# One 512-wide value product per key block, compressed logits joined to the window's last matmul, and gates kept as their inverses

## Chip, cores and metric

The kernel runs on one core of one Trainium2 chip. The metric is the time on the device in microseconds (us) of one execution; the times below are those of the kernel before, and the profile is of one further execution. TensorE is called PE, VectorE DVE, ScalarE ACT, GpSimd POOL, SyncE SP.

## What is computed

A transformer block over 1,024 tokens of width 1,024, in fp32: RMS norm, one projection (`w_in`), an mLSTM mixer and a sparse-attention mixer side by side, two gated branch products, an output product, and a gated feed-forward part. The change lies in the attention mixer, whose core is, for each block of queries:

```python
lc  = einsum(qb, kc_) + bias           # 63 compressed keys
p_c = masked_softmax(lc, ...);   o_c = einsum(p_c, vc_)
ls  = einsum(qb, k_g) + bias_s         # selected blocks: all keys up to the query
p_s = masked_softmax(ls, ...);   o_s = einsum(p_s, v_g)
lw  = einsum(qb, k_wb) + bias          # window of 512 keys
p_w = masked_softmax(lw, ...);   o_w = einsum(p_w, v_wb)
out = gb[0] * o_c + gb[1] * o_s + gb[2] * o_w     # gb = sigmoid(gate_in)
```

With 1,024 tokens and 16 blocks to select out of 16, "selected" means every key up to the query. There are 8 heads of width 64 in two groups of four; a group shares its keys and values.

## The kernel before

**Split numbers.** PE multiplies in a short format (fp32r), so fp32 operands are cut into a high part (a copy rounded to fp32r) and a low part (the rest). Projections take three matmuls per 128 rows of the contraction (`mm3`: high*high, high*low, low*high), each 512 columns wide. In the attention the two parts of the queries stand above one another in one tile (`QA`, 64 rows each), as do copies of the keys (`KH`, `KL`), so logits take two matmuls: `QA` with `KH`, then with `KL`. The values carry both parts side by side (`VHL`, and `VHC` for the compressed ones), so that rows 0 to 63 of the output are the product with the high part and rows 64 to 127 with the low part.

**Stages around the change.** B2 (about 313 to 383 us of the span) makes the queries: four tiles `nq`, each two halves of 24 matmuls, evicted by ACT (`snq`), cut by DVE (`hnq`, `lnq`) and stored through SP (`d_qh`, `d_ql`). Beside it `compress` makes the compressed keys `KHC`, `KLC` and values `VHC`. After the first tile, `load_pair(0)` loads what the attention of the first two heads needs: the queries `QA` and the keys `KH`, `KL` through POOL's DMA queue, the bias rows `FB`, `FW` through SP's. SP also loads the raw weights of the tiles to come (`raw`), and the compression's second weights (`w`).

C (383 to 708 us) is the attention. A unit is one pair of heads `p` and one block of 128 queries `i`; 32 units run, `i` in the order 0, 7, 1, 6, 2, 5, 3, 4 for each `p`. Per unit:

- `s_job`: logits of the window (`w`, up to 5 blocks of 128 keys), of the compressed keys (`c`, both heads in one job), of the selected keys (`s`, i+1 blocks). Each job takes one of two PSUM tiles `S` of two banks; DVE adds the bias and takes the row's extreme (`low`), ACT takes exp and the row sum (`exp`).
- `scale`: DVE makes gate / sum (`rs`: maximum, reciprocal, product with the gate `GT`), then DVE or ACT multiplies the rows with it.
- `t_job`: PE transposes two blocks of both heads into PSUM (`T`), ACT copies the high part out (`TH`), DVE subtracts for the low part (`TL`), and `pv` multiplies: per block one matmul with `TH`, one with `TL`, 256 columns each, summed in one half of the bank `obank`; units alternate between the halves.
- `out_copy`: ACT copies the 128 x 256 sums out (`os`), SP stores them to `d_yn`.

The order of all this is written by a planner in the kernel's own code (`Op`, `queues`, `ready`), which simulates PE, ACT and DVE with assumed durations; where PE would stand still for more than 120 ns it inserts a step of three matmuls (`d`) of the merge tiles, projections that need nothing of the attention. Nine of the sixteen merge tiles lie in C. `load_pair` for the next pair is called when the last logits of a pair are done; K tiles change only between pairs 1 and 2.

D (from 708 us) first makes the seven merge tiles left, 10.9 us each. Within them `load_y` is stepped, four steps to a tile: it loads `d_ym` and `d_yn` through SP, DVE adds the two `d_yn` sources (high and low values), ACT and DVE cut the sum into `YH` and `YL`, the operands of the branch products that begin at 785 us. In each tile ACT also evicts two halves and, in the fourth step, copies the next tile's weights (`whi`); POOL subtracts (`wlo`). Every engine's queue is in order.

Of the kernel before, what the change touches and what calls it, by code (L numbers as in the profile page):

```python
# [14 lines left out]
P = 128  # L15
T = 1024
# [15 lines left out]
FX = 1152  # L32
NEG = -1.0e30
# [124 lines left out]
def body(ctx, tc, a, out, stop=None, dbg=None):  # L158
# [45 lines left out]
    d_yn = [[tc.dram_tile([P, T], F32, name=f"d_yn{z}{j}") for j in range(4)] for z in range(2)]  # L204
# [137 lines left out]
    with ExitStack() as sa:  # L342
# [222 lines left out]
        def gates():  # L565
# [69 lines left out]
            nc.scalar.activation(GT[:, :, 0:24], GT[:, :, 0:24], AF.Sigmoid)  # L635
            nc.scalar.preload_act_table_set(EXPLN)
# [167 lines left out]

    def load_pair(p):
# [27 lines left out]
    with ExitStack() as sb:  # L833
# [73 lines left out]
        driver(b2_dense(), compress())  # L907
        if "VHC" in dbg:
# [9 lines left out]
    def merge_tile(j, sp, psp, bufs, tag="mg", tbufs=2):  # L918
# [8 lines left out]
    with ExitStack() as sc:  # L927
# [14 lines left out]
        def s_job(u, kind, r):  # L942
# [10 lines left out]
            if kind == "c":  # L953
                n8, nn = 8 * i + 8, ncmp(i)
                e = cp.tile([P, 2, P], F32, name=f"E{u}c", tag="Ec", bufs=3)
                nc.gpsimd.memset(e[:, :, nn:P], 0.0)
                EX[u, "c"] = e
                for q in range(2):
                    o = s[:, 64 * q:64 * q + n8]
                    nc.tensor.matmul(o, QA[2 * p + q][:, cs], KHC[:, g, 0:n8], start=True, stop=False)  # L960
                    nc.tensor.matmul(o, QA[2 * p + q][:, cs], KLC[:, g, 0:n8], start=False, stop=True)
                y0 = 31 + 16 * (56 - 8 * i)
                rows_ = [(e[:, q, 0:nn], s[:, 64 * q:64 * q + nn], FB[2 * p + q][:, y0:y0 + 16 * (nn - 1) + 1:16], q, 0)
                         for q in range(2)]
                cost = 4 * 107.0
            else:
                b = 1 if kind == "s" else 2
                n, k0 = (P * (i + 1), 0) if b == 1 else (P * nwin(i), P * max(0, i - 4))
                kh, kl = KS[g, b - 1]
                q_ = QA[2 * p + r]  # L970
                cost = 0.0
                for c0 in range(0, n, 512):
                    m = min(512, n - c0)
                    nc.tensor.matmul(s[:, c0:c0 + m], q_[:, cs], kh[:, k0 + c0:k0 + c0 + m], start=True, stop=False)
                    nc.tensor.matmul(s[:, c0:c0 + m], q_[:, cs], kl[:, k0 + c0:k0 + c0 + m], start=False, stop=True)
                    cost += 2 * max(107.0, m / 2.4)
                e = cp.tile([P, T if b == 1 else 640], F32, name=f"E{u}{kind}{r}", tag="E" + kind, bufs=4)
                EX[u, kind, r] = e
                if b == 1 or i < 4:
                    bias = FB[2 * p + r][:, 896 - P * i:896 - P * i + n]  # L980
                else:
# [938 lines left out]
```

## Time and profile before

| | |
|---|---|
| three runs | 1622.4 us median (1619.43 to 1623.4) |
| profiled execution, its time | 1624.57 us |
| its span, first to last instruction | 1622.8 us |
| PE, DVE, ACT busy in the span | 97%, 66%, 46% |
| PE, DVE, ACT busy in C | 98%, 83%, 79% |
| mean granted PE clock | 0.991 |

Busy shares of PE count matmuls that overlap, so the distance from one matmul's start to the next is the better measure of its cost. The feed-forward part after D is not touched.

### The profile page before, as it was taken

The numbers are of one execution on the slowest core, as the hardware profiler recorded it, in microseconds if no ns is written. First come the engines' busy times: TensorE is split into PE (matmuls) and PEld (weight loads), VectorE is DVE, ScalarE is ACT, GpSimd is POOL, SyncE is SP. The second block draws the span as 40 slices with busy tenths as digits, with TensorE's granted clock in tenths as the row PEclk, the third lists the DMA queues.
The fourth block names the chain that finished last, engine by engine and source line by source line (L and its number), as shares of the span: only waits on it lengthen the run. The fifth ranks groups of instructions, "written<-read, shape, count | busy, mean of one in ns | idle before, by whom it ended". The sixth has DMA issues, their size and how long they took to land.

```text
span 1622.8 us, 22113 instructions
## 1 busy us (share of the span) xinstructions
PE 1572.2 (97%) x7938; PEld 1327.5 (82%) x7938; DVE 1066.4 (66%) x2276; ACT 746.6 (46%) x1561; POOL 204.5 (13%) x225
## 2 busy tenths in 40 slices
PE   6999999989999999999999998999999999999997
PEld 6876888878989888988887887888888888888876
DVE  6456553245888687952355378666676666978996
ACT  5225455325878687853334344333333333454443
POOL 4002333310102110012000014000000000000130
PEclk9999999999999999999999999999999999999999
DMA  8003532782233422154447222222332223741202
GB/s 251 7 22 97 150 116 96 240 242 70 67 101 82 125 66 82 40 173 148 143 139 255 74 85 85 78 87 89 118 103 78 79 78 104 285 166 42 98 7 104
DMA packets 143773, 181.43 MB, mean 112 GB/s; under 512 B 10414, under 2 KB 100944, under 8 KB 143664
## 3 DMA queue, kind: packets, MB, share of 16 engines
q1 hardware_dynamic: 137440, 157.31, 31.5%
q0 software_dynamic: 5888, 22.06, 4.8%
q8 instruction: 62, 1.02, 0.3%
q10 hardware_dynamic: 336, 0.66, 0.1%
q14 instruction: 47, 0.39, 0.1%
HBM read 137.95 MB, written 49.90 MB: 116 GB/s over the span
## 4 chain that ended last, share of the span: by engine, by line
PE 82%; DVE 4%; DMA 3%; ACT 1%; issue 1%; SPq 0%; POOL 0%; DVEq 0%; ACTq 0%
PE PS L271 14%; PE PS L272 14%; PE PS L270 14%; PE d L270 6%; PE d L272 6%; PE d L271 6%; PE T L1043 4%; PE obank L1063 2%; PE obank L1065 2%; PE br L270 1%; PE br L271 1%; PE br L272 1%; DMA raw<-in_w_in 1%; PE pn L696 1%; DMA q<-d_yn 0%
## 5 line engine op out<-in xcount | busy, mean ns | idle before, releaser
L270 PE MATMUL d<-UTH,whi 128*128 128x512 f32 x576 | 235.1, 408 | 3.4 <-ACT snq L846 2.4
L272 PE MATMUL d<-UTH,wlo 128*128 128x512 f32 x576 | 227.1, 394 | 1.1 <-POOL wlo L249 1.1
L271 PE MATMUL d<-UTL,whi 128*128 128x512 f32 x576 | 226.1, 393 | 0.0
L1421 DVE TENSOR_TENSOR sl<-PS,sl 128x512 f32<-128x512 f32 x182 | 124.0, 688 | 100.2 <-PE PS L272 98.4
L272 PEld LDWEIGHTS d<-UTH,wlo 128*128 128x128 f32 x576 | 108.9, 189 | 26.1 <-POOL wlo L249 1.9
L270 PEld LDWEIGHTS d<-UTH,whi 128*128 128x128 f32 x576 | 109.2, 190 | 21.9 <-ACT snq L846 3.0
L249 POOL TENSOR_TENSOR wlo<-raw,whi 128x1024 fp32r<-128x1024 f32 x31 | 76.2, 2458 | 402.5 <-ACT whi L247 308.2
L271 PEld LDWEIGHTS d<-UTL,whi 128*128 128x128 f32 x576 | 109.6, 190 | 17.6
L1052 DVE TENSOR_TENSOR TL<-T,TH 128x512 fp32r<-128x512 f32 (+1 forms) x184 | 103.7, 583 | 20.9 <-ACT TH L1048 19.5
L1048 ACT ACTIVATE TH<-T 128x512 fp32r<-128x512 f32 (+1 forms) x184 | 90.8, 511 | 34.4 <-PE T L1043 31.6
L1421 DVE TENSOR_TENSOR sl<-sl,sl 128x512 f32<-128x512 f32 (+1 forms) x113 | 77.3, 691 | 18.3 <-ACT sl L1424 12.9
L1424 ACT ACTIVATE sl<-sl 128x512 f32<-128x512 f32 (+1 forms) x85 | 53.5, 631 | 69.8 <-PE PS L271 47.6
L1063 PE MATMUL obank<-TH,VHL 128*128 128x256 f32 x264 | 76.4, 312 | 0.0
L1424 ACT ACTIVATE wh<-sl 128x512 fp32r<-128x512 f32 x61 | 38.5, 631 | 81.9 <-PE PS L271 71.6
L1421 POOL TENSOR_TENSOR acc<-acc 128x512 f32<-128x512 f32 x6 | 9.2, 1548 | 503.5 <-DVE acc L1421 503.4
L1065 PE MATMUL obank<-TL,VHL 128*128 128x256 f32 x264 | 68.5, 282 | 0.0
L270 PE MATMUL PS<-q 128*128 128x512 f32 x172 | 66.9, 389 | 0.0
L271 PE MATMUL PS<-q 128*128 128x512 f32 x172 | 66.9, 389 | 0.0
L272 PE MATMUL PS<-q 128*128 128x512 f32 x172 | 66.9, 389 | 0.0
L1383 DVE TENSOR_TENSOR q<-br,q 128x512 f32<-128x512 f32 x32 | 21.9, 688 | 67.3 <-ACT q L1376 47.0
L1424 ACT ACTIVATE q<-sl 128x512 fp32r<-128x512 f32 x74 | 43.4, 624 | 46.5 <-PE PS L271 29.1
L1421 DVE TENSOR_TENSOR q<-sl,q 128x512 fp32r<-128x512 f32 x72 | 50.3, 736 | 2.9 <-ACT q L1424 2.9
(1418 smaller groups left out, 4302.0 us busy)
## 6 DMA issues: line engine op xcount, KB each, us to landing
raw<-in_w_in SPq DMA_DIRECT2D x40, 512.0 KB, 4.7
ra<-in_w_gate SPq DMA_DIRECT2D x22, 512.0 KB, 5.3
d_gu<-sl SPq DMA_DIRECT2D x44, 256.0 KB, 2.1
q<-d_mg SPq DMA_DIRECT2D x32, 256.0 KB, 3.2
d_rep<-d_row POOLq DMA_DIRECT2D x8, 960.0 KB, 10.0
sl<-d_gu SPq DMA_DIRECT2D x15, 512.0 KB, 5.3
sl<-in_w_down SPq DMA_DIRECT2D x15, 512.0 KB, 5.2
ra<-in_w_up SPq DMA_DIRECT2D x11, 512.0 KB, 3.8
```

The costliest lines, as they stand in the source:

```text
L249: eng.tensor_tensor(lo, v, cast32(hi), ALU.subtract)
L270: nc.tensor.matmul(ps, ah, bh, start=first, stop=False)
L271: nc.tensor.matmul(ps, ah, bl, start=False, stop=False)
L272: nc.tensor.matmul(ps, al, bh, start=False, stop=last)
L1043: nc.tensor.transpose(pt[:, z, P * r:P * r + P], e, ident)
L1048: nc.scalar.activation(hl[0][:, 0:m], pt[:, 0:m], AF.Copy)
L1052: nc.vector.tensor_tensor(hl[1][:, 0:m], pt[:, 0:m], cast32(hl[0])[:, 0:m], ALU.subtract)
L1063: nc.tensor.matmul(po, vv, th[:, z, :], start=(st[1] == 0), stop=False)
L1065: nc.tensor.matmul(po, vv, tl[:, z, :], start=False, stop=(st[1] == st[2]))
L1383: nc.vector.tensor_tensor(sg[b], ps, sg[b], ALU.mult)
L1421: return pl.step(alts, lambda e: ENG[e].tensor_tensor(out_(), x(), y(), alu), reads, writes, **kw)
L1424: return pl.step((("ACT", cost),), lambda e: nc.scalar.activation(out_(), x(), fn), reads, writes, **kw)
```

## The change

- **Value product.** High and low parts stand side by side in one tile `TT` [block, high or low, 256]. `pv` does one matmul of 512 columns per block. The output is now 128 x 512 and fills the bank, so all units take turns with it: the first `pv` of a unit depends on the `out_copy` of the unit before (was: two before). `os` is 512 wide in one buffer (was three of 256), `d_yn` doubles to 8 MB, and `load_y` sums four sources instead of two, in 16 half tiles of 512 columns instead of 8 tiles of 1,024 (10 steps become 18).
- **Compressed logits.** The K tiles of the window (`KH1`, `KL1`) are laid out in blocks of 192: 128 keys, then the 64 compressed keys of the group, repeated behind each block by POOL (`behind`). The last matmul pair of a window job is 192 wide, and its tail is the compressed logits. The `c` job is gone. K loads for these two tiles write pieces of 128 elements instead of whole rows of 1,024.
- **Gates.** `GT` is inverted once; `rs` is one maximum-and-product and one reciprocal, two DVE operations instead of three.
- **Room.** `sl` and `st` in B2 and `mg` in C go from two buffers to one.
- The planner's assumed durations follow.

```diff
+KB = 192
-    d_yn = [[tc.dram_tile([P, T], F32, name=f"d_yn{z}{j}") for j in range(4)] for z in range(2)]
+    d_yn = [[tc.dram_tile([2 * P, T], F32, name=f"d_yn{z}{j}") for j in range(4)] for z in range(2)]
...
+            nc.vector.reciprocal(GT[:, :, 0:24], GT[:, :, 0:24])
...
+    def behind(g):
+
+        for t_, c_ in zip(KS[g, 1], (KHC, KLC)):
+            nc.gpsimd.tensor_copy(t_[:, :, P:KB], c_[:, g, None, :].to_broadcast([P, NT, KB - P]))
...
-                kh = kq.tile([P, T], F32R, name=f"KH{g}{j}", tag=f"KH{j}", bufs=1)
+                m = KB if j == 1 else P
+                kh = kq.tile([P, NT, m], F32R, name=f"KH{g}{j}", tag=f"KH{j}", bufs=1)
...
-                nc.gpsimd.dma_start(kh[0:64, :], d_kh[j][gs, :])
...
+                for t_, d_ in ((kh, d_kh), (kl, d_kl)):
+                    for z in range(2):
+                        nc.gpsimd.dma_start(t_[64 * z:64 * z + 64, :, 0:P], d_[j][gs, :].rearrange("p (b c) -> p b c", c=P))
...
+            if g > 0:
+                behind(g)
...
-                    lo = bp.tile([P, 512], F32R, name=f"l{nm}{j}{half}", tag="sl", bufs=2)
-                    st = bp.tile([P, 512], F32, name=f"s{nm}{j}{half}", tag="st", bufs=2)
+                    lo = bp.tile([P, 512], F32R, name=f"l{nm}{j}{half}", tag="sl", bufs=1)
+                    st = bp.tile([P, 512], F32, name=f"s{nm}{j}{half}", tag="st", bufs=1)
...
+                nw = nwin(i)
+                n, o0 = P * nw, P if nw == 4 else 0
+                if nw > 1:
+                    logits(s[:, o0:o0 + n - P], lambda k: k[:, i + 1 - nw:i, 0:P], False)
+                logits(s[:, o0 + n - P:o0 + n - P + KB], lambda k: k[:, i, :], True)
...
-                nc.vector.tensor_scalar(rs, sm, 1.0e-30, None, ALU.max)
+                nc.vector.scalar_tensor_tensor(rs, sm, 1.0e-30, gt, ALU.max, ALU.mult)
                 nc.vector.reciprocal(rs, rs)
-                nc.vector.tensor_tensor(rs, rs, gt, ALU.mult)
...
-                    nc.tensor.matmul(po, vv, th[:, z, :], start=(st[1] == 0), stop=False)
                     st[1] += 1
-                    nc.tensor.matmul(po, vv, tl[:, z, :], start=False, stop=(st[1] == st[2]))
+                    nc.tensor.matmul(obank, vv, hl[0][:, z].rearrange("p x c -> p (x c)"), start=(st[1] == 1), stop=(st[1] == st[2]))
...
-                if first and u >= 2:
-                    dp.append(("OC", u - 2))
+                if first and u >= 1:
+                    dp.append(("OC", u - 1))
...
-            for k in range(10):
+            for k in range(18):
...
+                for src in ([d_ym[j]] if j < 4 else [d_yn[z][j - 4][P * x:P * x + P, :] for x in range(2) for z in range(2)]) if j < 8 else []:
```

How the order of instructions moves, at three places. The first is PE at the start of C: `S0w`, `S0c`, `S0s` are the logits of unit 0, `d` is a merge tile. Before:

```order
L974 MATMUL S0w_3228<-KH_2880,QA_2874 128x128
L975 MATMUL S0w_3228<-KL_2881,QA_2874 128x128
L974 MATMUL S0w_3232<-KH_2880,QA_2877 128x128
L975 MATMUL S0w_3232<-KL_2881,QA_2877 128x128
L270 MATMUL d_0_3210<-UTH,whi_3128 128x512
L271 MATMUL d_0_3210<-UTL,whi_3128 128x512
L272 MATMUL d_0_3210<-UTH,wlo_3129 128x512
L960 MATMUL S0c_3245<-KHC,QA_2874 128x8
L961 MATMUL S0c_3245<-KLC,QA_2874 128x8
L960 MATMUL S0c_3245<-KHC,QA_2877 128x8
L961 MATMUL S0c_3245<-KLC,QA_2877 128x8
L974 MATMUL S0s_3253<-KH_2886,QA_2874 128x128
```

The same place on PE now:

```order
L971 MATMUL S0w_3231<-KH_2881,QA_2875 128x192
L972 MATMUL S0w_3231<-KL_2882,QA_2875 128x192
L971 MATMUL S0w_3237<-KH_2881,QA_2878 128x192
L972 MATMUL S0w_3237<-KL_2882,QA_2878 128x192
L271 MATMUL d_0_3213<-UTH,whi_3129 128x512
L272 MATMUL d_0_3213<-UTL,whi_3129 128x512
L273 MATMUL d_0_3213<-UTH,wlo_3130 128x512
L971 MATMUL S0s_3253<-KH_2887,QA_2875 128x128
L972 MATMUL S0s_3253<-KL_2888,QA_2875 128x128
```

The four `c` matmuls are gone, and the window's last pair grows from 128 to 192 columns.

The second place is PE between the last two units: the transposes (`T`) of unit 31 and its first value product (`obank`). Before, the products of unit 31 go into the other half of the bank:

```order
L1043 MATMUL T_1_7696<-cst,E31w_7522 128x128
L1043 MATMUL T_1_7696<-cst,E31w_7565 128x128
L1043 MATMUL T_1_7696<-cst,E31w_7522 128x128
L1043 MATMUL T_1_7696<-cst,E31w_7565 128x128
L270 MATMUL d_1_7434<-UTH,whi_6711 128x512
L271 MATMUL d_1_7434<-UTL,whi_6711 128x512
L272 MATMUL d_1_7434<-UTH,wlo_6712 128x512
L1043 MATMUL T_2_7715<-cst,E31w_7522 128x128
L1043 MATMUL T_2_7715<-cst,E31w_7565 128x128
L1063 MATMUL obank<-TH_0_7701,VHL 128x256
L1065 MATMUL obank<-TL_0_7711,VHL 128x256
```

Now, where the first row is unit 30's last product and the last row unit 31's first, which waits for the copy of the bank:

```order
L1071 MATMUL obank<-TT_4_7051,VHL 128x512 x2
L1053 MATMUL T_1_7074<-cst,E31w_6896 128x128
L1053 MATMUL T_1_7074<-cst,E31w_6908 128x128
L1053 MATMUL T_1_7074<-cst,E31w_6896 128x128
L1053 MATMUL T_1_7074<-cst,E31w_6908 128x128
L271 MATMUL d_1_7083<-UTH,whi_6488 128x512
L272 MATMUL d_1_7083<-UTL,whi_6488 128x512
L273 MATMUL d_1_7083<-UTH,wlo_6489 128x512
L1053 MATMUL T_2_7089<-cst,E31w_6896 128x128
L1053 MATMUL T_2_7089<-cst,E31w_6908 128x128
L1071 MATMUL obank<-TT_0_7072,VHL 128x512 x2
```

Six transposes and one step of `d` stand between the two. After unit 31's last product 12 matmuls of `d` are left now; before, none was.

The third place is ACT in D: the merge tiles' evictions (`q` from `d`), the copies `YH`, and the next tile's weights (`whi`). Before, all of `load_y` ends within the third of the seven tiles:

```order
L266 ACTIVATE YH<-q_0_2_7808 128x512 x2
L247 ACTIVATE whi_7897<-raw_7802 128x1024
L266 ACTIVATE YH<-q_0_2_7808 128x512 x2
L922 ACTIVATE q_5_0_7789<-d_0_7873,COLS 128x512
L266 ACTIVATE YH<-q_1_3_7809 128x512 x2
L266 ACTIVATE YH<-q_4_1_7807 128x512 x2
L922 ACTIVATE q_5_0_7789<-d_1_7918,COLS 128x512
L266 ACTIVATE YH<-q_0_2_7808 128x512 x2
L247 ACTIVATE whi_7982<-raw_7877 128x1024
L266 ACTIVATE YH<-q_1_3_7809 128x512 x2
```

Now it ends in the fifth; these are the rows of the fourth and the fifth:

```order
L267 ACTIVATE YH<-q_0_2_7189 128x512
L248 ACTIVATE whi_7439<-raw_7326 128x1024
L267 ACTIVATE YH<-q_1_3_7190 128x512
L932 ACTIVATE q_5_0_7170<-d_0_7412,COLS 128x512
L267 ACTIVATE YH<-q_4_1_7188 128x512
L267 ACTIVATE YH<-q_0_2_7189 128x512
L932 ACTIVATE q_5_0_7170<-d_1_7463,COLS 128x512
L267 ACTIVATE YH<-q_1_3_7190 128x512
L248 ACTIVATE whi_7531<-raw_7416 128x1024
L267 ACTIVATE YH<-q_4_1_7188 128x512
```

Two `whi` now stand behind copies of sums of four (the third and the seventh of the eight such half tiles); before, one stood behind the third of the four sums of two.

## Rows read from the trace of the kernel before

**Rows 1.** Windows: stretch, busy us of each engine (instructions), PE clock, DMA share, GB/s.

```profile
358.00:369.00 11.00, 7.25 (x23) 5.59 (x23) 6.97 (x21) 1.06 (x1) 0.00 (x0) 0.53 0.84 241
383.00:708.00 325.00, 317.98 (x2121) 285.26 (x2120) 270.36 (x904) 257.11 (x675) 37.29 (x61) 1.00 0.30 75
708.00:785.00 77.00, 76.33 (x337) 62.87 (x336) 18.14 (x20) 23.69 (x37) 17.51 (x7) 1.00 0.55 176
```

**Rows 2.** Timeline of PE in C: start us, us, engine, line, tile, shape.

```profile
521.42 0.28 PE L1065 MATMUL obank<-TL,VHL 128*128 128x256 f32 x1
...
522.13 0.28 PE L1065 MATMUL obank<-TL,VHL 128*128 128x256 f32 x1
...
522.61 0.27 PE L960 MATMUL S15c<-KHC,QA 128*128 128x40 f32 x1
...
523.06 0.37 PE L1063 MATMUL obank<-TH,VHL 128*128 128x256 f32 x1
...
524.51 0.22 PE L974 MATMUL S15s<-KH,QA 128*128 128x128 f32 x1
...
524.68 0.45 PE L974 MATMUL S15s<-KH,QA 128*128 128x512 f32 x1
...
526.09 0.39 PE L270 MATMUL d<-UTH,whi 128*128 128x512 f32 x1
...
526.55 0.40 PE L272 MATMUL d<-UTH,wlo 128*128 128x512 f32 x1
```

**Rows 3.** The bank's instructions: count, ns min/median/max, first and last start.

```profile
L1063 PE MATMUL obank<-TH,VHL x264: 277/283/368, 389.7 to 706.2; 128*128 128x256 f32 x132
```

**Rows 4.** Groups by line in C: busy us, mean ns, idle before.

```profile
L1005 DVE TENSOR_TENSOR rs<-rs,GT 128x4 f32<-128x4 f32 x64 | 12.8, 199 | 2.2
```

**Rows 5.** Timelines of PE and ACT at C's end; idle before and releaser in brackets.

```profile
702.20 0.41 PE L1043 MATMUL T<-cst,E31c 128*128 128x128 f32 x2 [0.72 <-DVE TL L1052]
...
706.30 0.38 PE L1065 MATMUL obank<-TL,VHL 128*128 128x256 f32 x1
...
706.72 0.38 ACT L1071 ACTIVATE os<-obank 128x256 f32<-128x256 f32 x1 [0.93 <-PE obank L1065]
...
707.16 0.50 PE L270 MATMUL d<-UTH,whi 128*128 128x512 f32 x1 [0.47 <-ACT os L1071]
```

**Rows 6.** B2: two pieces of the ending chain, then timelines of ACT and PE.

```profile
334.25 21.21 DMA raw<-in_w_in
...
359.46 4.61 DMA w<-in_w_cmp
...
355.48 1.06 ACT L247 ACTIVATE whi<-raw 128x1024 fp32r<-128x1024 f32 x1 [8.90 <-DMA raw<-in_w_in]
...
357.34 0.50 PE L270 MATMUL d<-UTH,whi 128*128 128x512 f32 x1 [1.94 <-ACT snq L846]
...
364.20 1.19 PE L887 MATMUL ph<-fl,w 128*128 128x126 f32 x4 [3.75 <-DMA w<-in_w_cmp]
```

**Rows 7.** DMA queues from 338 to 348 us: packets, MB, share of 16 engines.

```profile
q0 software_dynamic: 625, 2.06, 84.2%
q1 hardware_dynamic: 822, 0.56, 42.4%
```

**Rows 8.** The store of `d_ql` issued at 338.0 us: us from issue to landing.

```profile
DMA to landing us min/median/max: 18.7/18.7/18.7
```

**Rows 9.** D: timelines of DVE, POOL and PE, and a DMA issue (KB, us to landing).

```profile
728.32 1.22 DVE L1354 TENSOR_TENSOR q<-q 128x1024 f32<-128x1024 f32 x1 [3.56 <-DMA q<-d_yn]
...
731.46 1.22 DVE L1354 TENSOR_TENSOR q<-q 128x1024 f32<-128x1024 f32 x1
...
738.02 3.16 POOL L249 TENSOR_TENSOR wlo<-raw,whi 128x1024 fp32r<-128x1024 f32 x1 [14.41 <-ACT whi L247]
...
741.23 0.50 PE L272 MATMUL d<-UTH,wlo 128*128 128x512 f32 x1 [0.67 <-POOL wlo L249]
...
q<-d_yn SPq DMA_DIRECT2D x8, 512.0 KB, 7.2
```

More of the change, by code (lines that the diff above doesn't have):

```diff
@@ L907, in body @@
         driver(b2_dense(), compress())
+        behind(0)
         if "VHC" in dbg:
@@ L952, in s_job @@
             s = psC.tile([P, T], F32, name=f"S{u}{kind}{r}", tag="S", bufs=2)
[L953 to L961, printed above, removed]
-                y0 = 31 + 16 * (56 - 8 * i)
[L963 to L981, printed above, removed]
-                    bias = FW[2 * p + r]
-                rows_ = [(e[:, 0:n], s[:, 0:n], bias, r, b)]
@@ new lines, in s_job, with logits @@
+            b = 1 if kind == "s" else 2
+            kh, kl = KS[g, b - 1]
+            q_ = QA[2 * p + r]
+            e = cp.tile([P, T if b == 1 else 640], F32, name=f"E{u}{kind}{r}", tag="E" + kind, bufs=4)
+            EX[u, kind, r] = e
+            f = FB[2 * p + r]
+            def logits(o, k_, last):
+                nc.tensor.matmul(o, q_[:, cs], k_(kh), start=True, stop=False)
+                nc.tensor.matmul(o, q_[:, cs], k_(kl), start=False, stop=True)
+            if b == 1:
+                n, o0 = P * (i + 1), 0
+                for c0 in range(0, i + 1, 4):
+                    m = min(4, i + 1 - c0)
+                    logits(s[:, P * c0:P * (c0 + m)], lambda k: k[:, c0:c0 + m, :], False)
+                rows_ = []
+            else:
+                nw = nwin(i)
[3 more added lines that the diff above has]
+                logits(s[:, o0 + n - P:o0 + n - P + KB], lambda k: k[:, i, :], True)
+                if r == 0:
+                    EX[u, "c"] = cp.tile([P, 2, P], F32, name=f"E{u}c", tag="Ec", bufs=3)
+                ec, nn = EX[u, "c"], ncmp(i)
+                nc.gpsimd.memset(ec[:, r, nn:P], 0.0)
+                y0 = 31 + 16 * (56 - 8 * i)
+                rows_ = [(ec[:, r, 0:nn], s[:, o0 + n:o0 + n + nn], f[:, y0:y0 + 16 * (nn - 1) + 1:16], r, 0)]
@@ L991, in exp @@
                     nc.scalar.activation(e_, e_, AF.Exp, bias=nx[:, q, b:b + 1], scale=-1.0, accum_out=sm[:, q, b:b + 1])
-            return cost, low, exp
+            return low, exp
         def scale(u, part):
@@ L1108, in build_s @@
             ops = {}
-            for k, r in (("w", 0), ("w", 1), ("c", 0), ("s", 0), ("s", 1)):
-                b = {"w": 2, "c": 0, "s": 1}[k]
+            for k, r in (("w", 0), ("w", 1), ("s", 0), ("s", 1)):
+                b = {"w": 2, "s": 1}[k]
                 box = {}
                 def emit(u=u, k=k, r=r, box=box):
-                    _, box["low"], box["exp"] = s_job(u, k, r)
-                n = 126 if k == "c" else (P * (i + 1) if b == 1 else P * nwin(i))
-                cost = 428.0 if k == "c" else 2 * sum(max(107.0, min(512, n - c) / 2.4) for c in range(0, n, 512))
+                    box["low"], box["exp"] = s_job(u, k, r)
+                if b == 1:
+                    n, parts = P * (i + 1), [min(512, P * (i + 1) - c) for c in range(0, P * (i + 1), 512)]
+                else:
+                    n, parts = P * nwin(i), [P * (nwin(i) - 1)] * (nwin(i) > 1) + [KB]
+                cost = 2 * sum(max(109.0, m / 2.4 + 13.0) for m in parts)
                 deps = []
@@ L1242, in place_dense @@
             dstate["gate"] = gate
-        todo_pair = {p: sum(1 for u in range(NU) if units[u][0] == p) * 5 for p in range(4)}
+        todo_pair = {p: sum(1 for u in range(NU) if units[u][0] == p) * 4 for p in range(4)}
         pair_at[0] = 2500.0
@@ L1354, in load_y @@
                         nc.vector.tensor_tensor(y, y, y2, ALU.add)
-                    for half in range(2):
-                        hs = slice(512 * half, 512 * half + 512)
-                        split_evict(YH[:, k - 2, hs], YL[:, k - 2, hs], y[:, hs])
+                    j, hs = (k - 2) // 2, slice(512 * (k % 2), 512 * (k % 2) + 512)
+                    split_evict(YH[:, j, hs], YL[:, j, hs], y)
                 yield
```

54 lines of the change are left out of this document (25 added, 29 removed).

## The prediction, made before the changed kernel ran

> **What bounds the kernel now.** I read the windows by stage first. In C PE is busy 318 of 325 us, DVE 270, ACT 257 [rows 1]. A busy PE counts matmuls that overlap, so I read next, in the timeline, how far apart matmuls start. In a run of value products seven starts lie 0.71 us apart from first to last, 0.118 us for one of 256 columns; 512-wide ones stand 0.23 us apart; the four `c` matmuls of a unit take 0.45 us up to the next product, though only 40 columns wide; a pair of 128-wide logits takes 0.17 us [rows 2]. These starts follow each other almost without gaps, so PE's own work sets C's length, and what is taken from it shortens C, as long as DVE (83%) and ACT (79%) keep up. The waits that remain are few; two sit at C's end, 0.72 and 0.47 us, where the merge steps have run out [rows 5].
>
> Then I followed the ending chain before C. In B2 a raw weight load issued at 334.25 us takes 21.2 us; ACT waits 8.9 us for it, PE 1.94 us for ACT's late eviction, and the second compression weights (`w`) are issued only at 359.46, since SP's queue is in order behind a store of the same late half; PE waits 3.75 us for them [rows 6]. In the 11 us around these waits PE's granted clock is 0.53, that is mostly the lower of its two levels, 1.2 instead of 2.4 GHz, while it stood idle and after [rows 1]. In D the only wait of PE is 0.67 us for `wlo` behind `load_y` [rows 9].
>
> **The change, part by part.**
>
> *Compressed logits.* Gone are 32 jobs of 0.45 us: 14.4 us of PE [rows 2]. Added: no row has a 192-wide pair; it lies between the 128-wide pair, 0.17, and two 256-wide matmuls, 0.24 us; I take 0.20. A 384-wide pair, likewise, lies between 0.24 and 0.46; I take 0.35. Of the 64 window jobs, 32 have five blocks and only swap a 128 for a 192 pair: +0.03 each, 1.0 us. For one to four blocks the job is cut in two where one pair did (0.17, 0.24, 0.35, 0.46 us become 0.20, 0.37, 0.44, 0.55): +0.34 us over the four, eight jobs of each: 2.7 us. Net -10.7 us (-12.5 to -8.2 with the pair at either end).
>
> *Value product.* 264 blocks [rows 3] and one compressed block per unit, 296 in all: 2 x 0.118 becomes 0.23, -2.0 us. One weight load goes, but not the columns, and columns are what is paid here. The Trainium skill ("TensorE: Matmul & The Clock Gate", Back-to-back issue gap) gives about 131 ns for a sustained 512-wide matmul and 81 ns for a 128-wide one. By that the 296 products would cost some 39 us and the gain would be thirty, not two. The dense runs here disagree: 0.23 us between starts [rows 2].
>
> *Turn-taking.* A unit's first product now waits for the copy of the whole bank. Seen at C's end: the last product starts at 706.30, ACT copies from 706.72 for 0.38 us, PE goes on at 707.16, 0.86 us later [rows 5]. With 512 columns the product is 0.11 longer and the copy about 0.6 (256 columns took 0.38, the 1,024-wide `whi` 1.06 [rows 6]), so 1.2 us, of which 0.23 is the product: 0.97 us of other work must stand between. In the new order I counted it at all 31 hand-overs, with the distances above and 0.11 for a transpose: the least is 1.0 us (unit 11), seven have under 1.5, most two to five. That is barely enough at seven places where ACT has something else queued; I take +1 us (0 to +4). Without the cover each would cost some 0.8.
>
> *End of C.* 12 matmuls of merge steps are left over now, so the two waits are filled: -1.2 us.
>
> *Gates, DVE and ACT.* 64 DVE operations of 0.2 us go, 12.8 us [rows 4]. The planner moves 14 row scalings from ACT to DVE (48 on ACT become 34), which ACT needs for copies that are 0.22 longer, 7 us. DVE and ACT both end a few us lower, as PE does: no gain by itself, cover for the rest. The inversion of `GT` is a single small operation in a stage where PE runs projections: nothing. The memsets double on POOL, which is busy 37 of 325 us [rows 1]: nothing.
>
> *K loads and single buffers in B2.* From 338 to 348 us two DMA queues compete: POOL's moved 625 packets of 3.3 KB on average, SP's 822 of 0.7 KB [rows 7]. They alternate nearly packet by packet, so the raw load, in small packets, gets a quarter of the bytes. Now half the K loads come in pieces of 512 bytes (128 elements), eight times as many. Alternating with those, the raw load should move as fast as they: the queries' 1 MB stands ahead of the keys in POOL's queue and is gone after 5 us at 2.06 MB in 10 us, near 343; at 82 packets per us (822 in 10 us) some 600 of the raw load's 1,024 pieces are then left. A small packet held an engine for about 0.08 us (42.4% of 16 engines for 10 us, over 822), so 600 alternating pairs take 4 to 6 us: it would land at 347 to 349 instead of 355.5. ACT's 8.9 us wait and PE's 1.94 us then go. Against it: the single `sl` buffer makes `lnq` wait for the store of the half before, which took 18.7 us [rows 8]; it is queued behind the same raw load and lands as much earlier, near 350, which `lnq` then waits for. The next `lnq` waits for the next store; so `w` is issued about 355 to 357 instead of 359.5, and PE, which would now arrive at 357.3, still waits some 2 to 3 us. Taken together 1.94 plus about 1.3 plus a part of the time lost at the lower clock: I take -4 us. Bounds: -8 if both waits and the low clock go; +3 if the raw load gets no faster and the single buffers delay `w` by another store (3 us).
>
> *K loads between pairs 1 and 2.* The new order has 18 us of PE work between the last logits that read the old keys and the first that read the new, more than the loads and two POOL copies need: nothing.
>
> *load_y.* A whole tile took 3.14 us of DVE and ACT in turn, 1.22 for its one add [rows 9]. A half tile now takes three adds of 0.61, the copy 0.62 and the subtraction 0.65: 3.2 us with hops, eight of them 25.6 us instead of 12.6. A merge tile (10.9 us) holds four, 12.8 us: the chain falls behind PE. The sources are issued after the second tile's last store, near 729.5, and land 7.2 us later [rows 9], at 737. The third copy ends at 745.9; `whi` 1.06, `wlo` 3.16 and hops follow: 750.5, needed at 751.3 (707.16 [rows 5] plus four tiles, plus two matmuls, since `wlo` is used by the third). The seventh ends at 758.7, its `wlo` at 763.3, needed at 762.2: 1.1 us of waiting in place of 0.67. The loads are 2 MB per half merge tile (5.45 us), 390 GB/s where D now moves 176 [rows 1], so they may lag a little. I take +1 us (-0.7 to +6).
>
> Sum: -10.7 - 2.0 + 1 - 1.2 - 4 + 1 = -15.9 us on the profiled execution's 1624.6, or 1608.7. That execution is 2.2 above the median, so on the median 1606.5.
>
> **Rivals.**
> - *B2 gives nothing.* The K loads' small pieces are no help, or the single buffers eat it: 1609 to 1614, 1611 likely. For it: no row shows pieces of 512 bytes in POOL's queue.
> - *DVE or ACT paces C.* PE's starts were dense only because merge steps filled every gap. DVE falls by 12.8 less about 6 for the scalings, so C shortens by some 6 us instead of 13: 1614. Against it: the waits on DVE and ACT in C are short.
> - *`load_y` becomes a wait.* If 8 MB come not in the 21 us that 390 GB/s need but at the 300 or so that the two queues of B2 moved together (2.62 MB in 10 us is 262), the chain ends 5 us later: 1612.
> - *The one bank stalls the units* (the slower side). If ACT reaches the copy late at most hand-overs, each costs up to 0.8 us plus what ACT is behind. Gains and losses balance when the mean uncovered wait over 31 hand-overs reaches about 0.55 us; at 0.8 it gives 1622.4 - 17 + 25 = 1630. Against it: the counted cover.
> - *Wide products overlap.* If a 512-wide product cost no more than a 256-wide one (0.118), 33 us more would go: 1573. That is the direction of the skill's page named above; the dense 512-wide rows speak against it.
>
> **Numbers.** The forecast as summed 0.52, its own range 1601 to 1611; B2 nothing 0.24; DVE or ACT 0.1; `load_y` 0.07; the one bank 0.05; overlap 0.01; no effect 0.01. The range that leaves out two in ten: 1599 to 1616. About 0.3%, 5 us, is what a measurement of this kernel tells from no change. Faster by more than that takes all cases but the bank, no effect and the upper tail of the others: 0.91; same 0.04; slower 0.05.
>
> **What would show it.** C (first `S0w` to the last `os`) 11 to 15 us shorter; products 0.23 apart; no `c` group; the first product of a unit with waits on `os` below 2 us in total; the raw load in B2 landing in 13 us rather than 21, and PE's wait for `w` below 3 us; one wait of PE on `wlo` of 1 us or so in D's sixth tile. The prediction is wrong if PE waits on `os` at most hand-overs, if the raw load still takes 20 us, if the 192-wide pairs cost more than 0.24, or if PE stands for many us at the entry to the branch products.

## The result and the profile after

| | before | after |
|---|---|---|
| median of six runs | 1622.46 us (1619.43 to 1623.4) | 1612.63 us (1610.84 to 1617.35) |
| profiled execution, its span | 1624.57, 1622.8 us | 1610.84, 1609.1 us |
| ratio after/before, 95% interval | | 0.9946, 0.993 to 0.9962 |

The change makes the kernel 9.8 us faster by the medians, 13.7 by the two profiled executions; the forecast was 15.9, that is 1606.5 us with a range of 1599 to 1616. Of the 3.9 us between the two measures, 2.1 are that before's profiled execution lies above its median, and 1.8 that the changed kernel's lies below its own.

By stages of the two traces (first `snq` of B2, first `S0w`, last `os`, first branch product): B2 is 1.8 us shorter (58.6 to 56.8), C 15.4 (323.8 to 308.4), D 4.6 longer (77.7 to 82.4). 12 of the merge matmuls, 2.7 us at 0.227, moved from C to D, so C gained 12.7 net and D lost 1.9. The stages ahead of B2 are 1.1 us shorter, those behind D differ by 0.1; the change doesn't touch them, but for the inversion of `GT` at 127 us, 1.4 us of DVE. "Net of the 12 merge matmuls" below means that these 2.7 us are counted with C.

Windows of the changed kernel: the stretch around the waits of B2, then C, then D (answers to [rows 1]).

```profile
356.00:367.00 11.00, 5.33 (x23) 4.39 (x22) 6.62 (x20) 1.69 (x2) 0.55 (x2) 0.69 0.83 240
380.00:688.00 308.00, 302.85 (x1729) 253.25 (x1728) 264.17 (x854) 249.20 (x658) 40.68 (x93) 1.00 0.39 91
688.00:771.00 83.00, 79.91 (x352) 65.52 (x351) 34.56 (x40) 25.92 (x39) 17.01 (x7) 1.00 0.67 219
```

In C, PE is still busy 98% of the time, and DVE and ACT, with shares of 86% and 81%, are nearer to it than before (83% and 79%). PE's timeline in C (answers to [rows 2]):

```profile
471.81 0.25 PE L971 MATMUL S11w<-KH,QA 128*128 128x192 f32 x1
...
472.01 1.04 PE L1053 MATMUL T<-cst,E9s 128*128 128x128 f32 x8
...
477.83 0.34 PE L971 MATMUL S11s<-KH,QA 128*128 128x384 f32 x1
...
478.18 1.08 PE L1071 MATMUL obank<-TT,VHL 128*128 128x512 f32 x4
479.11 0.60 PE L1053 MATMUL T<-cst,E10w 128*128 128x128 f32 x4
```

The 192-wide pair takes 0.20 us (471.81 to 472.01), the 384-wide pair 0.35, and four products of 512 columns 0.93, 0.23 each: the three prices of the forecast. The bank's instructions, and all waits of PE in C with total, number and longest (answers to [rows 3] and [rows 5]):

```profile
L1071 PE MATMUL obank<-TT,VHL x264: 388/398/506, 386.7 to 688.0; 128*128 128x512 f32 x132
L1078 ACT ACTIVATE os<-obank x32: 578/597/600, 390.2 to 688.4; 128x512 f32<-128x512 f32 x32
```

```profile
PE obank L1071 <- DVE TT L1061: 1.9, 2, 1.3
PE T L1053 <- DVE TT L1061: 1.7, 2, 1.5
PE d L271 <- ACT mg L932: 1.1, 2, 0.8
PE S26w L971 <- DVE nx L998: 0.2, 1, 0.2
```

PE never waits for `os`: the two waits of a product are for DVE's `TT`. (`mg` is ACT's eviction of a merge tile, `nx` DVE's work on the tile of logits before.) A copy of the bank takes 0.60 us, as estimated. Of the three operations of `rs` two are left (answer to [rows 4]):

```profile
L1014 DVE SCALAR_TENSOR_TENSOR rs<-sm,GT 128x4 f32<-128x4 f32 x64 | 12.0, 187 | 3.2 <-ACT E18c L1002 0.7 <-ACT E14c L1002 0.7 <-ACT E23c L1002 0.7
L1015 DVE RECIPROCAL rs<-rs 128x4 f32<-128x4 f32 x64 | 11.2, 174 | 2.2
```

B2, in the ending chain: start, length, what (answers to [rows 6] and [rows 8]); then ACT's split of the raw weights that SP issued at 333.02.

```profile
337.01 11.68 DMA d_ql<-lnq
348.78 0.78 DVE lnq L857
349.58 6.72 DMA d_ql<-lnq
356.40 0.69 DVE lnq L857
357.09 0.25 DVE fl L892
357.49 4.47 DMA w<-in_w_cmp
```

```profile
347.12 1.06 ACT L248 ACTIVATE whi<-raw 128x1024 fp32r<-128x1024 f32 x1 [1.55 <-DMA raw<-in_w_in]
```

The raw load is ready after 14.1 us, not 21.2, and PE's wait of 1.94 us behind ACT is gone. But the chain now runs over two stores: each `lnq` waits until the store of the half before has read the single `lo` buffer. `w` is issued at 357.49, and PE, which comes earlier now, waits 5.7 us for it, not 3.75. The queues from 338 to 348 us (answers to [rows 7]):

```profile
q0 software_dynamic: 1987, 1.75, 104.7%
q1 hardware_dynamic: 1037, 0.91, 47.6%
```

SP's queue moves 0.91 MB where it moved 0.56: 1.9 packets of POOL to one of SP now, where it was 0.8, but smaller ones.

D: PE's two waits, then DVE's chain of adds and POOL's subtraction, at an earlier tile (answers to [rows 9]).

```profile
746.71 0.50 PE L271 MATMUL d<-UTH,whi 128*128 128x512 f32 x1 [1.24 <-ACT whi L248]
...
749.30 0.50 PE L273 MATMUL d<-UTH,wlo 128*128 128x512 f32 x1 [1.85 <-POOL wlo L250]
```

```profile
727.04 2.14 DVE L1366 TENSOR_TENSOR q<-q 128x512 f32<-128x512 f32 x3
729.88 0.69 DVE L268 TENSOR_TENSOR YL<-q,YH 128x512 fp32r<-128x512 f32 x1 [0.70 <-ACT YH L267]
730.49 4.22 DVE L1366 TENSOR_TENSOR q<-q 128x512 f32<-128x512 f32 x3
```

```profile
730.87 2.55 POOL L250 TENSOR_TENSOR wlo<-raw,whi 128x1024 fp32r<-128x1024 f32 x1 [13.38 <-ACT whi L248]
```

Three adds take 2.14 us, but 4.22 when POOL's `wlo` starts among them: the one that starts at 731.21 takes 2.77 us, not 0.69, and ends at 733.98, 0.55 us after POOL. A half tile takes 3.45 us, since DVE also stands 0.70 us for ACT's copy in each. For the loads of `d_yn` DVE waits once in all of D, 2.1 us ahead of the first add.

### The profile page after: what moved, and what is told of

Same layout as the page of the kernel before. It is cut to its first block, busy times and chain, and to the rows that moved or that the text cites. A ratio compares the mean times of both kernels' runs of the same rounds, so it can differ in the third digit from the quotient of the medians.

```text
span 1609.1 us, 21387 instructions
## 1 busy us (share of the span) xinstructions
PE 1557.4 (97%) x7562; PEld 1296.3 (81%) x7562; DVE 1074.7 (67%) x2247; ACT 741.4 (46%) x1547; POOL 209.6 (13%) x261
## 4 chain that ended last, share of the span: by engine, by line
PE 81%; DVE 5%; DMA 3%; ACT 2%; issue 1%; SPq 0%; POOL 0%; DVEq 0%; ACTq 0%
PE PS L271 15%; PE PS L272 15%; PE PS L273 15%; PE d L271 6%; PE d L273 6%; PE d L272 6%; PE obank L1071 4%; PE T L1053 4%; PE br L273 1%; PE br L271 1%; PE br L272 1%; DMA d_ql<-lnq 1%; DVE q L1366 1%; DMA q<-d_yn 1%; PE pn L698 1%
## 5 line engine op out<-in xcount | busy, mean ns | idle before, releaser
L1061 DVE TENSOR_TENSOR TT<-T,TT 128x512 fp32r<-128x512 f32 (+1 forms) x184 | 104.0, 581 | 22.8 <-ACT TT L1058 21.5
L1058 ACT ACTIVATE TT<-T 128x512 fp32r<-128x512 f32 (+1 forms) x184 | 91.2, 510 | 28.9 <-PE T L1053 24.3
L1071 PE MATMUL obank<-TT,VHL 128*128 128x512 f32 x264 | 89.7, 424 | 1.9 <-DVE TT L1061 1.9
L1432 DVE TENSOR_TENSOR wh<-sl,wh 128x512 fp32r<-128x512 f32 x59 | 41.4, 702 | 13.9 <-ACT wh L1435 13.9
```

Of the source, the lines that this page charges most:

```text
L1058: nc.scalar.activation(hl[0][:, 0:m, 0], pt[:, 0:m], AF.Copy)
L1061: nc.vector.tensor_tensor(hl[0][:, 0:m, 1], pt[:, 0:m], cast32(hl[0])[:, 0:m, 0], ALU.subtract)
L1071: nc.tensor.matmul(obank, vv, hl[0][:, z].rearrange("p x c -> p (x c)"), start=(st[1] == 1), stop=(st[1] == st[2]))
L1432: return pl.step(alts, lambda e: ENG[e].tensor_tensor(out_(), x(), y(), alu), reads, writes, **kw)
```

## Experiments

All are edits of the changed kernel.

**The changed kernel again** (`after_again`). 

> The changed kernel once more, unedited. If its times are the same from run to run, the median is 1611 to 1614 us and the trace shows PE waiting 5 to 6 us for the second compression weights in B2 and 3 us in D, as in the first trace. If the wider spread of its times (1610.8 to 1617.4 in the first six) comes from transfers that happen to collide, one of these two waits differs from the first trace by more than 2 us.

Measured: 1611.78 us (1610.36 to 1613.49), 0.9941 of before (0.9926 to 0.9956). B2 takes 57.7 us, C 309.4. C's 1.1 us more are a wait of PE that the first trace lacks, for the next pair's queries:

```profile
PE S24w L971 <- DMA QA<-d_ql: 1.1, 2, 0.7
```

In D the two waits are 1.5 and 1.9 us, much as in the first trace, yet D takes 84.3 us, not 82.4. The window behind them says why:

```profile
750.00:755.00 5.00, 3.49 (x9) 2.78 (x10) 3.39 (x3) 2.24 (x4) 1.46 (x1) 0.68 0.05 19
```

The granted clock is 0.68 here; after the waits eight matmuls start 0.43 us apart, the lower of the two levels, not 0.23: 1.6 us more. Of the traces below, the seven with both waits (1.2 us or more for `whi`, 1.9 for `wlo`) show it too; the first trace, the quickest of its six runs, is the only one of nine without it. None of the four where these waits are shorter or absent shows it. Behind D it is the other way round: there this execution is 2.9 us shorter than the first (835.4 us for 838.3). A wait of PE in the branch stage is 1.0 us instead of 2.4, and the granted clock behind it stays at 1.00, where the first trace shows 0.79 from 858 to 866 us. So the low clock in D alone doesn't explain where an execution lies: what the first one escaped in D it paid further on.

The first trace is also at the lucky end in B2. In the nine traces that leave B2 as it is, B2 takes 56.8 to 59.2 us, 57.7 in the middle; 56.8 is the first trace's. D takes 84.1 to 84.9 us in the three traces below that leave it and C's order as they are (`w_early`, `two_buffers`, `gates_order`), against 82.4.

**The second compression weights earlier** (`w_early`).

```diff
...
+            w1s = [[w1_load(0, 0), w1_load(0, 1)], [w1_load(1, 0)]]
...
+                    if j == 0 and o == 7:
+                        w1s[1].append(w1_load(1, 1))
```

`w1_load` issues one half of a compression's weights.

> The second compression weights are issued earlier on SP: the first half at once, beside those of the first compression, the second half after the eighth of the first compression's matmuls, so neither stands behind a store of the single sl buffer. Theory (w is late only because of its place in SP's queue): PE's 5.7 us wait for w goes, B2 is 4 to 5.7 us shorter, C and D stay: 1607 to 1609 where the changed kernel is at 1612.6. Rival (the stores and the single buffers limit B2 whatever w does): PE waits for evictions of the projections instead, and under 1.5 us is gained, 1611 or more.

Measured: 1610.2 us (1605.93 to 1610.77), 0.9926 (0.9909 to 0.9942). B2 is 54.1 us, 2.6 shorter than in the first trace, 3.6 than in the middle one. Between the two theories: the wait for `w` is gone, another takes half its place.

```profile
PE ph L899 <- DVE fl L895: 2.9, 1, 2.9
```

The compression's operand `fl` stands behind `lnq` in DVE's queue, and `lnq` still waits for the store:

```profile
358.36 0.69 DVE L857 TENSOR_TENSOR lnq<-snq,hnq 128x512 fp32r<-128x512 f32 x1 [6.79 <-DMA d_ql<-lnq]
358.98 1.27 DVE L895 TENSOR_SCALAR fl<-KX,COLS 128x126 f32<-128x126 f32 x5
```

**Two buffers for the queries' halves** (`two_buffers`).

```diff
-                    lo = bp.tile([P, 512], F32R, name=f"l{nm}{j}{half}", tag="sl", bufs=1)
-                    st = bp.tile([P, 512], F32, name=f"s{nm}{j}{half}", tag="st", bufs=1)
+                    st = bp.tile([P, 512], F32, name=f"s{nm}{j}{half}", tag="st", bufs=2)
...
-                    nc.vector.tensor_tensor(lo, st, cast32(hi), ALU.subtract)
+                    nc.vector.tensor_tensor(st, st, cast32(hi), ALU.subtract)
...
-                    nc.sync.dma_start(dl[:, hs], cast32(lo))
+                    nc.sync.dma_start(dl[:, hs], st)
```

> The low part of the queries is subtracted in place, into the tile that held the sum, which gets two buffers in the room of lo and st: no lnq waits for the store before. Theory (the 5.7 us that PE waits for w in B2 are the two stores of the single buffer, 11.7 and 6.7 us, one behind the other): the wait falls under 2 us, B2 is 4 to 6 us shorter, 1606 to 1608.5 where the changed kernel is at 1612. Rival (w is late because the K loads fill the DMA engines, whatever the buffers): the wait stays above 4 us, 1611 or more.

Measured: 1610.42 us (1608.04 to 1612.58), 0.9928 (0.9916 to 0.994); B2 is 55.2 us. The waits for stores are gone and `w` is issued at 350.76, but now it takes twice as long; the chain and PE's wait:

```profile
331.93 14.27 DMA raw<-in_w_in
...
350.76 8.76 DMA w<-in_w_cmp
```

```profile
PE ph L895 <- DMA w<-in_w_cmp: 4.3, 1, 4.3
```

So the stores explain `w`'s late issue, 6.7 us; but `w` now takes 8.76 us instead of 4.47, which gives 4.3 of them back, and PE's wait is 1.4 us shorter, not gone. By the sign named beforehand, a wait above 4 us, the rival holds, though not by its reason. The queues while `w` is under way, 350.8 to 359.5 us:

```profile
q1 hardware_dynamic: 3447, 2.33, 98.4%
q0 software_dynamic: 160, 0.46, 17.2%
```

What `w` shares the engines with is mostly SP's own queue (raw weights, stores, `w`'s other half), and only the tail of POOL's K loads. The raw load takes 14.27 us with two buffers as well, so its speeding up doesn't come from the single buffers. Of the change's edits in B2 the K loads' pieces remain; they were not tried alone, so that they made the raw load faster is argued, not shown.

**load_y begun earlier** (`y_early`).

```diff
                 if z % 4 == 1:
                     next(ly, None)
+                    if j == NMC:
+                        next(ly, None)
```

> In the first merge tile of D load_y makes two steps where it made one, so the first load of d_yn is issued some 10 us earlier and the chain of adds ends near 742 instead of 751 us. Theory (the two waits in D, 1.2 us on whi and 1.9 on wlo, are the end of a chain that began too late): both go, D is 2.5 to 3 us shorter, 1609.5 to 1610 where the changed kernel is at 1612.6. Rival (the chain's steps are each too long, 3.45 us against 2.7 of PE, and POOL's subtraction collides with an add wherever it falls): the waits move to another tile and under 1 us is gained.

Measured: 1613.13 us (1610.78 to 1617.76), 0.9951 (0.9934 to 0.9968). The rival holds: the chain ends 7 us earlier, but in every tile it falls behind again, and the waits stand one tile sooner (739.9 us), 2.5 us for `whi` and 3.0 for `wlo`. D takes 86.6 us, longer than without the edit.

**The subtraction in D on DVE** (`wlo_dve`).

```diff
-        yield from fm_tile(j_mg[j], psp, "D", bufs, evict, pool=True, mark=True)
+        yield from fm_tile(j_mg[j], psp, "D", bufs, evict, pool=j < NMC, mark=True)
```

> In D the weights' low part is subtracted by DVE instead of POOL (1.22 us where DVE did it in other stages). Theory (a DVE operation that starts beside POOL's subtraction stands until that is through: 2.77 instead of 0.69 us, twice in load_y's adds and twice in YL): no DVE operation of 512 columns in D is over 0.8 us, the chain gains about 0.9 us per merge tile and wlo comes about 1 us sooner after whi, so PE's two waits fall from 3.1 to under 1.5 us: 1610.5 to 1611.5 where the changed kernel is at 1612.6. Rival (the long adds wait for their operands' transfers): the 2.5 to 2.8 us operations stay, and with 1.2 us more on DVE per tile PE waits as long or longer: 1612.6 to 1614.

Measured: 1608.06 us (1607.79 to 1613.09), 0.9924 (0.9907 to 0.994). DVE and PE's waits in D:

```profile
747.15 1.23 DVE L250 TENSOR_TENSOR wlo<-raw,whi 128x1024 fp32r<-128x1024 f32 x1 [0.26 <-ACT whi L248]
748.30 2.13 DVE L1366 TENSOR_TENSOR q<-q 128x512 f32<-128x512 f32 x3
```

```profile
PE d L271 <- ACT whi L248: 1.0, 1, 1.0
PE d L273 <- DVE wlo L250: 0.5, 1, 0.5
```

No add in D takes over 0.69 us. The long ones were POOL's doing, not the transfers'. D takes 80.8 us at full clock, although DVE does more work. That the time lies below the theory's 1610.5 goes with the low clock, 1.6 us in `after_again`, which doesn't follow these shorter waits.

**The value product undone** (`two_products`).

```diff
-                    nc.tensor.matmul(obank, vv, hl[0][:, z].rearrange("p x c -> p (x c)"), start=(st[1] == 1), stop=(st[1] == st[2]))
+                    for x in range(2):
+                        nc.tensor.matmul(po, vv, hl[0][:, z, x], start=(st[1] == 1 and x == 0), stop=(st[1] == st[2] and x == 1))
...
-                if first and u >= 1:
-                    dp.append(("OC", u - 1))
+                if first and u >= 2:
+                    dp.append(("OC", u - 2))
...
```

> The changed kernel with the value product undone: two products of 256 columns per block into alternating halves of the bank, copies 256 wide, d_yn 4 MB and load_y with two sources again; joined logits, inverse gates and B2 stay. Theory (PE pays for columns, so the wide product is worth 2 us, and the four sources of load_y cost D 2 us and more): C is 1 to 3 us longer, D without its left-over merge steps 1.5 to 3 us shorter, together 1610 to 1613 where the changed kernel is at 1612. Rival (the wide product brings most of what the change gave): 1618 or more.

Measured: 1610.5 us (1608.61 to 1612.96), 0.9929 (0.9915 to 0.9943). C is 2.3 us longer net of the 12 merge matmuls, which are in C again; 1.1 of these 2.3 us are longer waits of PE (6.0 us in C for 4.9). D, likewise net, is 2.9 shorter, without a wait for weights. The wide product gains about what was forecast and D takes it back: by time the two kernels can't be told apart.

**The compressed logits undone** (`c_apart`): the `c` job of the kernel before, on the new K tiles.

```diff
...
+                for q in range(2):
+                    o = s[:, 64 * q:64 * q + n8]
+                    nc.tensor.matmul(o, QA[2 * p + q][:, cs], KHC[:, g, 0:n8], start=True, stop=False)
+                    nc.tensor.matmul(o, QA[2 * p + q][:, cs], KLC[:, g, 0:n8], start=False, stop=True)
...
```

> The changed kernel with the compressed logits as a job of their own again, four matmuls of up to 64 columns and one S tile per unit, and the window's last pair 128 wide; the K tiles keep their blocks of 192. Theory (C's length is PE's own work, 32 jobs of 0.45 us against 3.7 us for the wider and extra pairs): C plus the merge steps left over is 10 to 13 us longer, 1622 to 1625 where the changed kernel is at 1612. Rival (other waits take it up, DVE's or ACT's): under 6 us, 1618 or less.

Measured: 1629.74 us (1626.91 to 1631.32), 1.0045 (1.0032 to 1.0058): slower than before. C is 14.2 us longer net of the 12 merge matmuls. PE's own work accounts for some 9.3: the 32 jobs take 13.0 us from start to start, less 3.7 for the wider and the extra pairs. Of the rest, 4.2 us are waits of the `c` job for its turn with the two `S` tiles (for `nx`, DVE's work on the tile before), the longest of them here; 3.4 us of C are at the lower clock as well.

```profile
PE S30c L982 <- DVE nx L1007: 2.2, 1, 2.2
...
PE S22c L982 <- DVE nx L1007: 1.6, 1, 1.6
```

**The gates undone** (`gates_undone`, then `gates_order` with the planner's cost left at 400).

```diff
-            nc.vector.reciprocal(GT[:, :, 0:24], GT[:, :, 0:24])
...
-                nc.vector.scalar_tensor_tensor(rs, sm, 1.0e-30, gt, ALU.max, ALU.mult)
+                nc.vector.tensor_scalar(rs, sm, 1.0e-30, None, ALU.max)
                 nc.vector.reciprocal(rs, rs)
+                nc.vector.tensor_tensor(rs, rs, gt, ALU.mult)
...
-                    rs = push(Op("DVE", 400.0, de, todo[0][0], (u, 2)))
+                    rs = push(Op("DVE", 600.0, de, todo[0][0], (u, 2)))
```

> The changed kernel with the gates as they were: three small DVE operations per scale step instead of two, 64 more of 0.2 us, 12.8 us of DVE in C. Theory (DVE is not what sets C's length): 1611 to 1614 where the changed kernel is at 1612, C within 1.5 us. Rival (after the change DVE paces C): C 4 us longer or more, 1616 and up.

> The three-operation gates again, but with the planner's assumed cost left at the changed kernel's, so that PE's and ACT's instructions stand in exactly the changed kernel's order and only DVE has 64 operations more. Theory (most of what the undone gates cost, 11 us in C, comes by the order: the planner, told of a busier DVE, spends its 12 spare merge matmuls earlier and has none where C ends): 1612 to 1616, C at most 4 us longer than the changed kernel's. Rival (DVE's 12.8 us themselves are on PE's path now): 1620 or more, C 8 us longer or more.

Measured: `gates_undone` 1626.46 us (1618.82 to 1630.09), 1.0021 (1.0009 to 1.0034), `gates_order` 1617.35 (1615.82 to 1618.64), 0.9969 (0.9957 to 0.9981). The first theory fell: C is 11.3 us longer net of the 12 merge matmuls. In the changed kernel's order it is 4.8 us longer, between the two expectations but nearer to the theory: 64 operations on DVE are on PE's path for little more than a third of their 12.8 us, and the other 6.6 come with the order. The last 30 us of C show what the order does, first `gates_undone`, then the changed kernel:

```profile
672.30:702.30 30.00, 24.30 (x126) 17.31 (x124) 25.38 (x77) 24.05 (x61) 0.00 (x0) 0.94 0.14 27
```

```profile
658.00:688.00 30.00, 28.44 (x158) 22.58 (x157) 24.48 (x64) 20.97 (x52) 2.45 (x1) 1.00 0.26 62
```

In the first no merge matmul is left to fill the gaps, in the second there are 41, and PE is busy 4 us more. The end isn't all: at the turns from one pair to the next PE waits 4.3 us for loads, where the first trace of the changed kernel has no such wait and the second one of 1.1.

```profile
PE S16s L971 <- DMA KL<-d_kl: 1.7, 1, 1.7
PE S8w L970 <- DMA QA<-d_ql: 1.4, 1, 1.4
PE S24w L970 <- DMA QA<-d_ql: 1.2, 1, 1.2
```

That the order moved the merge steps away from there too was not tested.

**The bank copied twice** (`copy_twice`).

```diff
                         nc.scalar.activation(os_, obank, AF.Copy)
+                        nc.scalar.activation(os_, obank, AF.Copy)
```

> The changed kernel with the copy of the bank done twice in a row by ACT, so that the bank comes free about 0.6 us later at each of 31 hand-overs and ACT is busy 19 us longer in C; the planner doesn't know of it. Theory (one to five us of other PE work stand at every hand-over, so the bank's turn costs nothing): PE waits on os under 5 us in all, and the time is 1612 to 1618. Rival (the hand-overs are just covered): 31 times 0.6 us, 19 us longer, 1628 and more.

Measured: 1623.77 us (1619.31 to 1627.17), 1.0006 (0.9996 to 1.0016). C is 11.5 us longer, 0.6 of it the second copy at its very end, so the time is off both theories; the waits show which part holds:

```profile
PE T L1053 <- DVE TT L1061: 3.5, 7, 2.2
PE obank L1071 <- DVE TT L1061: 2.5, 2, 1.6
...
PE obank L1071 <- ACT os L1079: 0.8, 3, 0.3
```

Only 0.8 us is waited for the bank itself. All waits of PE in C are 8.1 us for 4.9, and 3.4 us are at the lower clock. About half of the 11.5 us shows in no wait: that it is many small delays behind ACT's 19 us, whose halves of `TT` come later, is argued. The hand-over is covered; ACT's queue as a whole isn't.

**Repairs together** (`best_dve`: the edits of `two_buffers`, `w_early` and `wlo_dve`; `best_pool`: the first two, and a line that adds the halves in C, with `d_yn` and `load_y` fitted to two sources).

```diff
...
                         nc.scalar.activation(os_, obank, AF.Copy)
+                        nc.gpsimd.tensor_tensor(os_[:, 0:256], os_[:, 0:256], os_[:, 256:512], ALU.add)
...
```

> Three repairs together: the low part in place with two buffers, w issued early, the weights' low part in D on DVE. If their gains add up (4 to 6 us in B2, 2 to 4 in D): 1602 to 1606, PE's waits in B2 under 1 us and in D under 2 us. If they overlap: not below the better of the single ones, 1607.

> The two repairs of B2, and in place of the one in D the two column halves of each unit's sum are added by POOL in C (32 additions of 256 columns), so d_yn is 4 MB and load_y sums two sources as in the kernel before. If POOL's additions are hidden in C: C as in the changed kernel, 308 us, D 2.5 us or more shorter, 1602 to 1606. If they hold up DVE's operations as POOL's subtraction does in D: C 3 us longer or more, 1606 to 1610.

Measured: `best_dve` 1601.11 us (1598.83 to 1602.68), 0.9868 (0.9855 to 0.988). The gains more than add up: B2 takes 49.3 us without a wait over 0.5, 8.4 less than the middle trace, where the two edits alone gave 3.6 and 2.5; each alone leaves the other's wait standing. D takes 80.6 us, and PE holds the full clock where it used to wait:

```profile
350.00:360.00 10.00, 10.00 (x50) 8.40 (x49) 6.66 (x20) 0.92 (x3) 2.59 (x4) 1.00 1.25 295
360.00:370.00 10.00, 10.00 (x58) 8.60 (x56) 3.46 (x5) 2.51 (x4) 0.00 (x0) 1.00 0.55 180
```

`best_pool` 1611.67 us (1610.06 to 1616.09), 0.994 (0.9927 to 0.9953): D is 78.6 us, 3.7 shorter, but C 10.5 longer. ACT and PE's waits in C:

```profile
ACT os L1082 <- DMA d_yn<-os: 9.0, 2, 8.2
```

```profile
PE d L271 <- ACT mg L936: 7.2, 2, 6.8
```

Neither expectation named this. At pair 2 POOL issues the K loads and makes two copies before its add, the stores of the sum go out among these loads, the single `os` waits for its stores, and ACT, in order, holds up everything behind it. PE's 6.8 us wait is followed by six matmuls 0.42 to 0.60 us apart, at the lower clock, 1.4 us more.

## Why the prediction was right, point by point

The forecast time was 6 us low and within the range, but above its own 1601 to 1611: 1612.6 lies where the rival "B2 gives nothing" stands, and that rival is nearly what happened. Two terms make up the miss. With the middle B2 (57.7) and a D of 84.3 as in the second trace, B2 gave 0.9 us, not 4, and `load_y` cost 3.8, not 1; with C's -12.7 that is -9.8, as much as the medians show. The kernel before has one trace, so this takes its stages for typical. That the profiled pair comes nearer, 13.7, is luck in part: B2 and D (net of the merge matmuls) are shorter in its second execution than in any other that leaves them unedited. The terms:

- *Compressed logits, -10.7.* Right. The pairs cost 0.20 and 0.35 us. The price of a job, 0.45, was read at one place; the 32 jobs of the kernel before take 13.4 us, 0.42 each, so that PE's work fell by 9.7. Undone, the job costs 14.2 in C, as the forecast didn't count its turn with the `S` tiles.
- *Value product, -2.0.* Right in mechanism, and about in size: 2.3 when undone, 1.1 of it in waits. The rival that wide products overlap is out, with 0.23 us between starts.
- *Turn-taking, +1.* Nothing was waited for `os`. The count was right: the least work between two units is 1.0 us, six hand-overs have under 1.5, and at the tightest the bank comes free 0.15 us ahead of the product. With a copy 0.6 us longer 0.8 us is waited in all. The rival of the stalling bank is out.
- *C's end, -1.2.* Right: where unit 31 waited 1.7 us and PE 0.47 behind its last product, unit 31 now waits 0.2 and nothing stands behind it. One wait of 1.3 us, for `TT`, is left in unit 30. C as a whole was forecast at -12.9 and came out at -12.7.
- *Gates, DVE and ACT: nothing by itself, cover for the rest.* The mis-sized step. "Cover" is right, since C came out as summed only with it, but it is no reserve to spare: 12.8 us on DVE alone cost 4.8 in C, with the plan that follows from it 11.3, and 19 us on ACT cost 11.5. The rival that DVE or ACT paces C, given 0.1, was close. Undoing the three edits one by one adds 14.2, 2.3 and 11.3 us to C (4.8 in the changed kernel's order), more than the 12.7 that they gain together: they lean on each other's room, as the waits for DVE's `nx` and `TT` suggest.
- *B2, -4.* Mis-sized: -1.8 in the first trace, -0.9 in the second and in the middle one of nine. The raw load did what was worked out (14.1 us for 13), and that `lnq` would wait for the store near 350 too (348.7). But a second store of 6.7 us followed, `w` was issued at 357.5, not at 355 to 357, and PE came 1 us sooner, at 356.4: it waited 5.7 us for the forecast 2 to 3. The window around it is at a clock of 0.69, not 0.53 [rows 1].
- *`load_y`, +1.* The place is right, D's sixth tile, and the size wrong: +1.9 in the first trace, +3.8 in the second. The rival that the transfers are slow is out as a mechanism: DVE waits for them once, 2.1 us, ahead of the first add. Its 300 GB/s stood in no row; beside the 262 named with it the chain would have ended some 10 us later, not 5. The chain was costed at 3.2 us a step from rows without POOL beside them; a step takes 3.45, and 2.1 more in each that meets `wlo`. A wait on `whi`, not foreseen, came ahead of the one on `wlo`, and the low clock behind both.

Still open: the share of the K loads' pieces in B2, tried by no kernel alone; where about half of `copy_twice`'s 11.5 us goes; and why the same wait is followed by the low clock in one execution and not in another.

## What to carry to other kernels

Work taken from one engine frees room on another only as long as nobody spends it: undo each part of a joint change by itself before calling one of them idle. A buffer given up for space became a wait for a store where two DMA queues were busy; here subtracting in place gave the second buffer back without more space. Where the order comes from a planner, an assumed duration moves filler work, and the price shows up far away: here at the stage's end, and perhaps at the pairs' turns. And take more than one trace before calling a stage's gain measured: between two executions of one kernel B2 differed by 0.9 us and D by 1.9.

## What the runs showed of the hardware

A DVE operation with two operands in SBUF that starts beside POOL's subtraction stands until that is through: 2.77 and 2.72 us, not 0.69, twice among the adds and, in two operations of `YL`, 2.46, not 0.69; with the subtraction on DVE none does. The Trainium skill ("SBUF — State Buffer", SBUF: two separate sides) states an exclusive lock between DVE with two SBUF inputs and a GpSimd operation that reads SBUF. The trace agrees: each of the four ends 0.55 us after POOL does. What the forecast lacked by it is the 2.1 us in each merge tile whose adds meet a `wlo`.

Two waits of PE of 3.1 us and more in all, 2.6 us apart, were followed by six to eleven matmuls at 0.43 us, the level of 1.2 GHz, in eight of nine traces; with waits of 1.0 and 0.5 us (`wlo_dve`) the granted clock stayed at 1.00. So nearly the same stall cost 1.6 us more in the second execution of the changed kernel than in the first.
